# Transposed products of a two-layer hybrid backbone: 512 weight columns per pass over four open PSUM tiles, in place of 256 over one

## The chip, the cores and the metric

One core of a Trainium2 chip runs the whole program. The metric is device time of one execution in microseconds (us); a lower time is better. The trace is one execution taken by the hardware profiler; TensorE is PE in its rows (its weight loads PEld), VectorE DVE, ScalarE ACT, GpSimd POOL and SyncE SP. "ACTq" is ACT's instruction queue, which also issues DMAs; each engine's queue is worked in the order in which it was written.

## The reference

512 tokens (256 of context, 256 latent), width 1024, two layers, each followed by a squared-ReLU MLP. Cut to what the change touches:

```
layer 0:  z, xbc, dt, q, k, v, lr, r = split(h @ w_in)
          y = ssd_scan(x, dt, B, C) both directions        # 16 heads of 64, chunks of 128 tokens
          o = gla_scan(q, k, v, gate) both directions      # 8 heads
          y = rmsnorm((y + D*x) * silu(z));  o = rmsnorm(o) * silu(r)
          out = concat(y, o) @ w_out
layer 1:  q, i, f, g, u = split(h @ w_in)
          o = gla_scan(silu(q), 1 - f, v = i, log f) both directions; s5 on u
          o = rmsnorm(o) * silu(g) ...
```

The change concerns z, v and r of layer 0, and v and g of layer 1: five products whose result is wanted with tokens on the partitions.

## The kernel before, in words

All weights come from HBM as fp32. `wtile` (line 210) loads a block of 512 KB into one of four buffers from the SP queue and splits it into a high part (`whi`, ACT, line 79) and a rest (`wlo`, DVE, line 86); `mm3` (line 100) then spends three matmuls on each pair of blocks: high by high, high by rest, rest by high. The activations `hhi`, `hlo` are split likewise.

There are two forms of product. `gemm_f` (line 319) holds a 128x128 block of weights in the array and moves 512 token columns. `gemm_t` (line 338), the one of this change, holds a block of activations (128 contraction rows by 128 tokens) and moves weight columns, so tokens come out on the partitions. Before, it takes 256 weight columns at a time: two weight blocks of four contraction tiles each, and for each pair of token blocks one PSUM tile (`psd`, a pool of four tiles of 128x512), whose halves are two token blocks of 256 columns. The whole contraction runs for one tile, `put` empties it, and the next tile follows. A product of 1024 columns for 512 tokens is 4 chunks of 96 matmuls; all five together are 1728 matmuls of 256 columns.

The order on each engine is made when the program is built, by a scheduler that works down the program's text and moves work ahead of what it holds to be late; the text itself interleaves generators. Three stages hold the work of the change:

- **SSD scan of layer 0** (some 160 to 288 us). `v_r_proj` (line 1029) makes v and r, a chunk per step; `run_out` (line 1048) takes one step for every second yield of `scan_out` (line 956). `scan_out` works on 4 chunks of tokens with 4 groups of heads each, 16 groups in all. For a group it fetches two blocks `R[0]`, `R[1]` (256 KB each, the cumulated decays, one for each direction, spread over all partitions) from DRAM by ACT's queue (line 977), adds a bias to `R[1]` with four ACT instructions (line 980), adds another to `R[0]` on DVE (line 981), selects between them into `R[0]` (DVE, line 982), takes the exponential (ACT, line 983), multiplies by the scores `Ssb` (DVE, line 984), and multiplies the result as the stationary operand (line 989). `R[0]` is free after that matmul, `R[1]` after the selection. Each has three buffers in the pool `ssd2`.
- **GLA of layer 0** (to 480 us). `z_proj` (line 1212) makes z; its steps are given out before each of the four pairs of heads by `ZN`. `gla_in` (line 1238) makes q and k by `gemm_f` and the decays and states by a chain over DVE and ACT.
- **HGRN of layer 1** (985 to 1250 us). `projs` (line 1549) places the chunks of q, v and g into slots -2 to 7 by `QP`, `VP` and `GP`.

In r and z, `put` computes silu: a bound on DVE that reads PSUM, three ACT steps of the sigmoid, and a product on DVE that reads the PSUM tile again, so the tile stays open until then.

Of the kernel before, what the change touches and what calls it, by code (L numbers as in the profile page):

```python
# [12 lines left out]
AF = mybir.ActivationFunctionType  # L13
# [4 lines left out]
P = 128  # L18
T = 512
# [9 lines left out]
NID = 8  # L29
DTM = 11  # L30
NF = 2
ZN = 3, 1, 2, 2
ADN = 0, 6, 11, 0
WA = 0, 1
QP = -2, 1, 2, 5
VP = -2, -1, 0, -1
GP = -1, 0, 4, 6
SP = -2, -1, 1, 3, 3, 5


def emit(tc, A, out):
# [18 lines left out]
    def tl(p, shape, tag, dt=F32, bufs=None):  # L60
        kw = dict(tag=tag, name=tag)
        if bufs is not None:
            kw["bufs"] = bufs
        return p.tile(list(shape), dt, **kw)

    def ps_d():
        return tl(pd, [P, T], "psd")
# [17 lines left out]
    def tt(eng, o, a, b, op):  # L85
        eng.tensor_tensor(out=o, in0=a, in1=b, op=op)  # L86

    def ts(eng, o, a, s1, op0, s2=None, op1=None):
        if op1 is None:
            eng.tensor_scalar(out=o, in0=a, scalar1=s1, scalar2=None, op0=op0)  # L90
        else:
            eng.tensor_scalar(out=o, in0=a, scalar1=s1, scalar2=s2, op0=op0, op1=op1)
# [7 lines left out]
    def mm3(o, l, r, start, stop):  # L100
        mm(o, l[0], r[0], start, False)
        mm(o, l[0], r[1], False, False)
        mm(o, l[1], r[0], False, stop)
# [86 lines left out]
    def sigmoid_(buf):  # L190
        act(buf, buf, AF.Exp, scale=-1.0)
        act(buf, buf, AF.Ln, bias=1.0)
        act(buf, buf, AF.Exp, scale=-1.0)
# [16 lines left out]
    def wtile(W, k0, kt, c0, n):  # L210

        raw = tl(wp, [P, kt, n], "wraw", bufs=RAW)
        Q.dma_start(out=raw, in_=W[k0 * P:(k0 + kt) * P, c0:c0 + n].rearrange("(k p) c -> p k c", p=P))
        return wsplit(raw, kt, n)
# [41 lines left out]
    def step(it, n=1):  # L256
        for _ in range(n):
            next(it, None)
# [78 lines left out]

    def gemm_t(W, c0, x, toks, put):

        w = [wtile(W, 4 * i, 4, c0, 256) for i in range(2)]  # L340
        for i, pair in enumerate(toks):
            ps = ps_d()
            for j, tok in enumerate(pair):
                t_ = slice(tok * P, (tok + 1) * P)
                for k in range(8):
                    wk = w[k // 4]
                    mm3(ps[:, 256 * j:256 * j + 256], (x[0][:, k, t_], x[1][:, k, t_]),
                        (wk[0][:, k % 4], wk[1][:, k % 4]), k == 0, k == 7)
            put(i, ps)

    xd = tc.dram_tile([8, P, T], F32, name="xd")
    xd2 = tc.dram_tile([8, P, 256], F32, name="xd2")
# [603 lines left out]
    def scan_out(c, hs):  # L956

        S_ps = ps_s()
        for g in range(4):
            mm(S_ps[:, g * P:(g + 1) * P], bT[:, g, c * P:(c + 1) * P], cT[:, g, c * P:(c + 1) * P])  # L960
        Ssb = tl(s2, [P, 4, P], "Ssb", bufs=1)
        act(Ssb, S_ps.rearrange("p (g i) -> p g i", g=4), AF.Copy)
        sdt = tl(s2, [P, 4, P], "y", bufs=2)
        tt(V, sdt, Ssb, ident.unsqueeze(1).to_broadcast([P, 4, P]), MUL)
        sd = tl(s2, [P, 4, 1], "sd")
        V.tensor_reduce(out=sd, in_=sdt, axis=mybir.AxisListType.X, op=ADD)
        dsk = tl(s2, [P, 4, 4], "dsk")
        tt(V, dsk, dtm[:, c, 32:48].rearrange("p (g h) -> p g h", g=4), sd.to_broadcast([P, 4, 4]), MUL)
        dsk = dsk.rearrange("p g h -> p (g h)")
        tt(V, dsk, dsk, dskip, ADD)  # L970
        for hf in range(2):
            yI = ps_s()
            for g in (2 * hf, 2 * hf + 1):
                R = []
                for d in range(2):
                    R.append(tl(s2, [P, 4, P], f"R{d}", bufs=3))
                    S.dma_start(out=R[d], in_=acd[d, 4 * g:4 * g + 4, c * P:(c + 1) * P].partition_broadcast(P))
                X = R[0]
                for h_ in range(4):
                    act(R[1][:, h_], R[1][:, h_], AF.Identity, bias=lnd[:, c, 32 + 4 * g + h_:33 + 4 * g + h_])  # L980
                tt(V, X, X, bcol(lnd, c, 4 * g, 4, P), ADD)
                V.copy_predicated(X, ms.bitcast(I32).unsqueeze(1).to_broadcast([P, 4, P]), R[1])
                act(X, X, AF.Exp)
                tt(V, X, X, Ssb[:, g].unsqueeze(1).to_broadcast([P, 4, P]), MUL)
                for h_ in range(4):
                    hh = 4 * g + h_
                    o_ = (g % 2) * 256 + h_ * 64
                    for q_ in (0, 64):
                        PE.matmul(yI[q_:q_ + 64, o_:o_ + 64], lhsT=X[:, h_, q_:q_ + 64], rhs=xtm[:, c, hh * 64:hh * 64 + 64], start=True, stop=True, skip_group_check=True, tile_position=(0, q_))
                yield  # L990
            xs = xtm[:, c, hf * T:(hf + 1) * T]
            xs3 = xs.rearrange("p (h d) -> p h d", h=8)
            tt(V, xs3, xs3, dsk[:, 8 * hf:8 * hf + 8].unsqueeze(2).to_broadcast([P, 8, 64]), MUL)
            tt(V, xs, xs, yI, ADD)
            for d in range(2):
                if hs[d] is None:
                    continue
                yX = ps_s()
                for g in range(2):
                    gg = 2 * hf + g  # L1000
                    mm(yX[:, 256 * g:256 * g + 256], cT[:, gg, c * P:(c + 1) * P], hs[d][:, gg * 256:gg * 256 + 256])
                t1 = tl(s2, [P, T], "y", bufs=2)
                tt(V, t1.rearrange("p (h d) -> p h d", h=8), yX.rearrange("p (h d) -> p h d", h=8),
                   bcol(eac, c, 32 * d + 8 * hf, 8, 64), MUL)
                tt(V, xs, xs, t1, ADD)

    def silu_ps(pl, ps, tag, bufs):

        sg = tl(pl, [P, T], tag, bufs=bufs)
        ts(V, sg, ps, -44.0, MAX)  # L1010
        sigmoid_(sg)
        tt(V, sg, sg, ps, MUL)
        return sg

    PAIRS = ((0, 1), (2, 3))

    def two(t):
        return t.rearrange("p (t c) -> p t c", t=2)
# [8 lines left out]

    ad = counted(ada_all(lambda: scr[0](), (0, 1), (0, 2)))
    def v_r_proj():
        for ch in range(4):  # L1030
            def put(i, ps, ch=ch):
                act(vtm[:, 2 * i:2 * i + 2, 256 * ch:256 * ch + 256], two(ps), AF.Copy)
            gemm_t(W0, 4128 + 256 * ch, h, PAIRS, put)
            yield
        for ch in range(4):
            def put(i, ps, ch=ch):
                sg = sr[:, 2 * i:2 * i + 2, 256 * ch:256 * ch + 256]
                ts(V, sg, two(ps), -44.0, MAX)
                sigmoid_(sg)
                tt(V, sg, sg, two(ps), MUL)  # L1040
            gemm_t(W0, 5184 + 256 * ch, h, PAIRS, put)
            yield

    fill = v_r_proj()
    f1 = state(0, 0, None)
    b1 = state(1, 1, None)
    step(fill)
    def run_out(c, hs):
        for i, _ in enumerate(scan_out(c, hs)):
            if i % 2 == 1:  # L1050
                step(fill)

    f2 = state(0, 1, f1)
    b2 = state(1, 0, b1)
# [155 lines left out]
    osq = tl(g1, [P, 4, 8], "osq")  # L1210

    def z_proj():
        for g in range(4):
            def put(i, ps, g=g):
                sg = silu_ps(g2, ps, "sg", 1)
                ys = xtm[:, 2 * i:2 * i + 2, 256 * g:256 * g + 256]
                tt(V, ys, ys, two(sg), MUL)
                for j in range(2):
                    S.activation(out=sg[:, 256 * j:256 * j + 256], in_=ys[:, j], func=AF.Square,
                                 accum_out=ssq[:, 2 * i + j, g:g + 1])  # L1220
            gemm_t(W0, 256 * g, h, PAIRS, put)
            yield
        rstd_small(ssq, 256)
        for c in range(4):
            y3 = xtm[:, c].rearrange("p (g f) -> p g f", g=4)
            tt(V, y3, y3, ssq[:, c].unsqueeze(2).to_broadcast([P, 4, 256]), MUL)
        yield
# [258 lines left out]
        tt(V, q_, q_, two(ps), MUL)  # L1486

    def v_proj(ch):
        def put(i, ps):
            act(vtm[:, 2 * i:2 * i + 2, 256 * ch:256 * ch + 256], two(ps), AF.Copy)  # L1490
        gemm_t(W1i, 1024 + 256 * ch, h, PAIRS, put)

    def g_proj(ch):
        def put(i, ps):
            g_ = sgl[:, :, 256 * ch:256 * ch + 256]
            ts(V, g_, two(ps), -44.0, MAX)
            sigmoid_(g_)
            tt(V, g_, g_, two(ps), MUL)
        gemm_t(W1i, 4096 + 256 * ch, h, ((2, 3),), put)

    def hgrn_in(hd_):
        def chain(d):
# [45 lines left out]

    def projs(slot):
        for f_, at in ((q_proj, QP), (v_proj, VP), (g_proj, GP)):  # L1550
            for ch in range(4):
                if at[ch] == slot:
                    f_(ch)
        for a_ in SP:
            if a_ == slot:
                step(s5)
# [137 lines left out]
```

## Time and profile before

| | us |
|---|---|
| median of 3 runs (1477.54 to 1480.27) | 1480.12 |
| the profiled execution | 1479.99 |
| its span, first to last instruction | 1478.3 |
| PE busy | 1424.7 (96%) |
| DVE busy | 945.8 (64%) |
| ACT busy | 682.5 (46%) |
| POOL busy | 328.0 (22%) |

1.7 us of the profiled execution lie around the span. Busy PE is not PE at its peak: a matmul counts from its start to its modelled end, and neighbours overlap, so the pace is read from counts in a stretch. The mean granted clock over the span is 0.988.

### The profile page before, as it was taken

The page shows a single profiled execution, that of the slowest core. Times are in us where ns is not written, and L with a number is a line of the kernel's source. Part 1 is how long each engine was busy: PE and PEld are TensorE (multiplying, and loading weights), DVE is VectorE, ACT ScalarE, POOL GpSimd, SP SyncE. Part 2 cuts the span into 40 slices and gives each one's busy share as a digit, 9 for nine tenths or more (in the row PEclk, how much of TensorE's full clock was granted, in tenths as well). Part 3 has the DMA queues.
Part 4 walks back from the last instruction along what each step waited for, and adds up shares of the span by engine and source line. Part 5 has one row for each costly group of instructions (what it writes and reads, how often), then busy time and mean ns, then how long its engine had stood idle before and what let it go on. Part 6 is the DMA issues. An engine that isn't in the chain of part 4 may idle for free.

```text
span 1478.3 us, 24336 instructions
## 1 busy us (share of the span) xinstructions
PE 1424.7 (96%) x9598; PEld 1211.4 (82%) x9598; DVE 945.8 (64%) x1600; ACT 682.5 (46%) x1313; POOL 328.0 (22%) x348
## 2 busy tenths in 40 slices
PE   7999999999989999999999999999999999999998
PEld 4788998888636889877877777899988888899998
DVE  4798688886755447745444834384786898655543
ACT  4566545475433235421322413362375687555532
POOL 2100000000000012394087840213511110044210
PEclk9999999999988999999999999999999999999999
DMA  9732545322266443465567566569645322565752
GB/s 332 193 100 72 139 121 138 93 58 72 97 220 181 143 114 84 150 186 172 156 202 210 171 193 183 148 207 192 172 115 146 113 93 68 156 188 170 208 177 84
DMA packets 291406, 222.43 MB, mean 150 GB/s; under 512 B 22646, under 2 KB 268844, under 8 KB 291292
## 3 DMA queue, kind: packets, MB, share of 16 engines
q1 hardware_dynamic: 253584, 184.84, 42.8%
q10 hardware_dynamic: 32140, 16.09, 4.6%
q0 software_dynamic: 5568, 19.96, 4.3%
q8 instruction: 75, 1.23, 0.4%
q14 instruction: 39, 0.32, 0.1%
HBM read 206.39 MB, written 14.46 MB: 149 GB/s over the span
## 4 chain that ended last, share of the span: by engine, by line
PE 68%; DVE 10%; DMA 8%; issue 5%; ACT 4%; POOL 3%; ACTq 0%; SPq 0%; DVEq 0%; POOLq 0%
PE psd L98 57%; PE pss L98 6%; DMA R<-acd 3%; PE pss L235 3%; PE pss L106 2%; DVE wlo L86 2%; DMA araw<-in_ada_w_dram 1%; DMA wraw<-in_ada_w_dram 1%; POOL cma L86 1%; DVE hL L134 1%; POOL cmb L86 1%; ACT whi L79 1%; DMA wraw<-in_ssd_gla_w_in_dram 1%; ACT hL L79 1%; POOL ph L86 1%
## 5 line engine op out<-in xcount | busy, mean ns | idle before, releaser
L86 DVE TENSOR_TENSOR wlo<-wraw,whi 128x1024 fp32r<-128x1024 f32 (+1 forms) x238 | 308.4, 1299 | 200.9 <-ACT whi L79 199.4
L79 ACT ACTIVATE whi<-wraw 128x1024 fp32r<-128x1024 f32 (+1 forms) x250 | 260.6, 1044 | 342.8 <-DMA wraw<-in_mlp_w_dram 164.6
L98 PE MATMUL psd<-hhi,wlo 128*128 128x512 f32 (+1 forms) x1112 | 381.7, 345 | 1.0 <-DVE wlo L86 1.0
L98 PE MATMUL psd<-hlo,whi 128*128 128x512 f32 (+1 forms) x1112 | 381.7, 345 | 0.8 <-DVE hlo L86 0.8
L98 PE MATMUL psd<-hhi,whi 128*128 128x512 f32 (+1 forms) x1112 | 379.8, 347 | 2.7 <-ACT hhi L79 2.7
L98 PEld LDWEIGHTS psd<-hhi,whi 128*128 128x128 f32 x1112 | 210.2, 191 | 35.7 <-ACT mr L79 5.0
L98 PEld LDWEIGHTS psd<-hhi,wlo 128*128 128x128 f32 x1112 | 211.8, 191 | 25.9 <-DVE wlo L86 2.4
L98 PEld LDWEIGHTS psd<-hlo,whi 128*128 128x128 f32 x1112 | 211.5, 191 | 24.7 <-DVE hlo L86 1.5
L98 PE MATMUL psd<-wlo,hhi 128*128 128x256 f32 x576 | 165.2, 287 | 2.8 <-DVE wlo L86 2.8
L98 PE MATMUL psd<-whi,hhi 128*128 128x256 f32 x576 | 164.9, 288 | 0.0
L98 PE MATMUL psd<-whi,hlo 128*128 128x256 f32 x576 | 164.5, 286 | 0.0
L98 PEld LDWEIGHTS psd<-wlo,hhi 128*128 128x128 f32 x576 | 111.1, 193 | 4.7 <-DVE wlo L86 3.0
L98 PEld LDWEIGHTS psd<-whi,hhi 128*128 128x128 f32 x576 | 110.7, 193 | 2.6 <-issue 1.3
L98 PEld LDWEIGHTS psd<-whi,hlo 128*128 128x128 f32 x576 | 111.0, 193 | 0.6 <-issue 0.2
L98 PE MATMUL psd<-hidh,whi 128*128 128x512 f32 (+1 forms) x288 | 107.7, 374 | 0.0
L98 PE MATMUL psd<-hidh,wlo 128*128 128x512 f32 (+1 forms) x288 | 105.7, 367 | 1.1 <-DVE wlo L86 1.1
L86 POOL TENSOR_TENSOR nsa<-nsa,nsq 128x256 f32<-128x256 f32 x28 | 26.0, 930 | 362.3 <-ACT nsq L79 361.9
L98 PE MATMUL psd<-hidl,whi 128*128 128x512 f32 (+1 forms) x288 | 105.6, 367 | 0.0
L95 DVE SCALAR_TENSOR_TENSOR xtm<-psd,mod,xtm 128x256 f32<-128x256 f32 x96 | 42.3, 476 | 72.4 <-PE psd L98 65.1
L98 PE MATMUL psd<-hl,whi 128*128 128x256 f32 x256 | 73.0, 285 | 0.0
L98 PE MATMUL psd<-hh,wlo 128*128 128x256 f32 x256 | 72.9, 285 | 0.0
L98 PE MATMUL psd<-hh,whi 128*128 128x256 f32 x256 | 72.4, 283 | 0.0
(438 smaller groups left out, 2475.1 us busy)
## 6 DMA issues: line engine op xcount, KB each, us to landing
wraw<-in_mlp_w_dram SPq DMA_DIRECT2D x128, 512.0 KB, 4.2
wraw<-in_ada_w_dram SPq DMA_DIRECT2D x80, 512.0 KB, 3.8
wraw<-in_ssd_gla_w_in_dram SPq DMA_DIRECT2D x48, 512.0 KB, 4.5
wraw<-in_hgrn_s_w_in_dram SPq DMA_DIRECT2D x43, 512.0 KB, 4.3
araw<-in_ada_w_dram SPq DMA_DIRECT2D x16, 512.0 KB, 11.3
R<-acd ACTq DMA_DIRECT2D x32, 256.0 KB, 4.6
wraw<-in_ssd_gla_w_out_dram SPq DMA_DIRECT2D x16, 512.0 KB, 4.7
wraw<-in_hgrn_s_w_out_dram SPq DMA_DIRECT2D x12, 384.0 KB, 3.2
```

The costliest lines, as they stand in the source:

```text
L79: ins = S.activation(out=out_, in_=in_, func=func, scale=scale, bias=bias)
L86: eng.tensor_tensor(out=o, in0=a, in1=b, op=op)
L95: eng.scalar_tensor_tensor(out=o, in0=a, scalar=s, in1=b, op0=op0, op1=op1)
L98: PE.matmul(o, lhsT=l, rhs=r, start=start, stop=stop, skip_group_check=True)
L106: PE.transpose(o, i, ident[:rows, :rows])
L134: V.tensor_tensor_scan(out=o, data0=rz[:n], data1=x, initial=0.0, op0=MUL, op1=ADD)
L235: PE.matmul(ps[32 * gg:32 * gg + 32], lhsT=cs[:, k], rhs=raw[:, g * T:(g + 1) * T], start=(k == 0), stop=(k == 7), skip_group_check=True, ...
```

## The change

`gemm_t` opens one PSUM tile for each token block (four, or two for g, which is for the latent tokens only), takes the contraction in four parts of two tiles with 512 weight columns, and goes over all token blocks with each part; a tile is handed to `put` in the last part. It is a generator that yields after each part, so v and r now have 16 steps in place of 8, and `run_out` takes one at each yield. The number and size of the weight loads stay (40 of 512 KB).

r's gate copies the PSUM tile to `sr` with ACT and finishes from SBUF with a tile `sg` of its own (two buffers in the pool `ssd2`); z's gate multiplies `xtm` by the PSUM tile before the sigmoid is ready and by the sigmoid afterwards. `R[0]` and `R[1]` go from three buffers each to two. The tables of steps and slots change with the number of chunks.

```diff
-ZN = 3, 1, 2, 2
+ZN = 4, 4, 1, 0
-VP = -2, -1, 0, -1
-GP = -1, 0, 4, 6
+VP = -2, -1
+GP = 0, 4
     def gemm_t(W, c0, x, toks, put):
-        w = [wtile(W, 4 * i, 4, c0, 256) for i in range(2)]
-        for i, pair in enumerate(toks):
-            ps = ps_d()
-            for j, tok in enumerate(pair):
+        pss = [ps_d() for _ in toks]
+        for q in range(4):
+            w = wtile(W, 2 * q, 2, c0, T)
+            for i, tok in enumerate(toks):
                 t_ = slice(tok * P, (tok + 1) * P)
-                for k in range(8):
-                    wk = w[k // 4]
-                    mm3(ps[:, 256 * j:256 * j + 256], (x[0][:, k, t_], x[1][:, k, t_]),
-                        (wk[0][:, k % 4], wk[1][:, k % 4]), k == 0, k == 7)
-            put(i, ps)
+                for k in range(2):
+                    kk = 2 * q + k
+                    mm3(pss[i], (x[0][:, kk, t_], x[1][:, kk, t_]), (w[0][:, k], w[1][:, k]), kk == 0, kk == 7)
+                if q == 3:
+                    put(i, pss[i])
+            yield
...
-                    R.append(tl(s2, [P, 4, P], f"R{d}", bufs=3))
+                    R.append(tl(s2, [P, 4, P], f"R{d}", bufs=2))
...
+            def put(i, ps):
+                sg = tl(s2, [P, T], "sg", bufs=2)
+                ts(V, sg, ps, -44.0, MAX)
+                act(sr[:, i, c5], ps, AF.Copy)
                 sigmoid_(sg)
-                tt(V, sg, sg, two(ps), MUL)
+                tt(V, sr[:, i, c5], sr[:, i, c5], sg, MUL)
...
-    step(fill)
+    step(fill, 2)
     def run_out(c, hs):
-        for i, _ in enumerate(scan_out(c, hs)):
-            if i % 2 == 1:
-                step(fill)
+        for _ in scan_out(c, hs):
+            step(fill)
...
+                sg = tl(g2, [P, T], "sg", bufs=1)
+                ys = xtm[:, i, T * ch:T * ch + T]
+                ts(V, sg, ps, -44.0, MAX)
+                tt(V, ys, ys, ps, MUL)
+                sigmoid_(sg)
+                tt(V, ys, ys, sg, MUL)
```

What the scheduler makes of it is seen in two places. The first is PE's queue at the end of the SSD scan. Before, the products of the 16 groups (`pss<-xtm,R`, line 989; the numbers tell the buffers apart) have projection work (`psd`) between them to the end; here are the last two groups:

```order
L98 MATMUL psd<-hlo,whi 128x512
L98 MATMUL psd<-hhi,wlo 128x512
L989 MATMUL pss<-xtm,R_2827 64x64 x8
L98 MATMUL pss<-H_2249,cT 128x256 x2
L98 MATMUL pss<-H_1556,cT 128x256
L989 MATMUL pss<-xtm,R_2847 64x64 x8
L98 MATMUL pss<-H_1556,cT 128x256
L98 MATMUL psd<-whi,hhi 128x256
```

In the changed kernel's queue, from the ninth group on:

```order
L98 MATMUL psd<-wlo,hhi 128x512
L98 MATMUL psd<-whi,hlo 128x512
L991 MATMUL pss<-xtm,R_2040 64x64 x8
L98 MATMUL pss<-H_1495,cT 128x256 x2
L98 MATMUL pss<-H_2014,cT 128x256 x2
L991 MATMUL pss<-xtm,R_2090 64x64 x8
L991 MATMUL pss<-xtm,R_2183 64x64 x8
L98 MATMUL pss<-H_1495,cT 128x256 x2
L98 MATMUL pss<-H_2014,cT 128x256 x2
L98 MATMUL pss<-cT,bT 128x128 x4
L991 MATMUL pss<-xtm,R_2237 64x64 x8
L991 MATMUL pss<-xtm,R_2316 64x64 x8
```

The remaining four groups follow in the same way, and only behind the sixteenth come further matmuls on `psd`: the last eight groups have no projection work between them.

The second place is ACT's queue for the same groups (here with buffer numbers; `R0` and `R1` are `R[0]` and `R[1]`, DMA is the issue of a copy). Before, the copies of three `R0` buffers stand together, a good way ahead of the instructions that need them:

```order
L977 DMA R0_1763<-acd_142 128x4x128 [waits DVE_49,PE_49]
L977 DMA R0_1918<-acd_142 128x4x128 [waits DVE_49,PE_49]
L977 DMA R0_1938<-acd_142 128x4x128 [waits DVE_49,PE_49]
L79 ACTIVATE R0_1763<-R0_1763 128x512 [waits DVE_49]
L977 DMA R1_2081<-acd_142 128x4x128 [waits Activation_49]
```

In the changed kernel, groups 11 to 13 (`R0_2183`, `R0_2237`, `R0_2316`):

```order
L79 ACTIVATE R0_2040<-R0_2040 128x512 [waits DVE_49]
L979 DMA R1_2185<-acd_142 128x4x128
L79 ACTIVATE R1_2185<-R1_2185,lnd_1400 128x128 [waits DMAHW3_49]
L79 ACTIVATE R1_2185<-R1_2185,lnd_1400 128x128 x3
L79 ACTIVATE Ssb_2030<-pss_2025 128x512 [waits PE_49]
L79 ACTIVATE R0_2090<-R0_2090 128x512 [waits DVE_49]
L979 DMA R1_2239<-acd_142 128x4x128 [waits DMAHW5_49]
L79 ACTIVATE R1_2239<-R1_2239,lnd_1400 128x128 [waits DMAHW5_49]
L79 ACTIVATE R1_2239<-R1_2239,lnd_1400 128x128 x3
L979 DMA R0_2183<-acd_142 128x4x128 [waits DVE_49,PE_49]
L979 DMA R0_2237<-acd_142 128x4x128 [waits DMAHW7_49,DVE_49,PE_49]
L79 ACTIVATE R0_2183<-R0_2183 128x512 [waits DVE_49]
```

A copy of an `R1` now stands directly ahead of the instructions that read it, and the copies of the two `R0` stand behind those.

## Rows read from the trace of the kernel before

**Rows 1.** The page: busy time by engine, and the chain that ended last.
```profile
PE 1424.7 (96%) x9598; PEld 1211.4 (82%) x9598; DVE 945.8 (64%) x1600; ACT 682.5 (46%) x1313; POOL 328.0 (22%) x348
...
PE 68%; DVE 10%; DMA 8%; issue 5%; ACT 4%; POOL 3%; ACTq 0%; SPq 0%; DVEq 0%; POOLq 0%
```

**Rows 2.** Windows: us, each engine's busy time (instructions), PEclk, DMA share, GB/s.
```profile
500.00:520.00 20.00, 20.00 (x91) 16.57 (x90) 8.73 (x13) 3.33 (x4) 0.00 (x0) 1.00 0.49 152
196.00:286.00 90.00, 85.61 (x761) 77.61 (x760) 76.12 (x122) 44.61 (x90) 0.99 (x2) 0.98 0.50 133
286.00:375.00 89.00, 86.16 (x634) 75.99 (x633) 64.07 (x95) 54.89 (x133) 0.00 (x0) 0.98 0.23 66
1017.00:1053.00 36.00, 36.00 (x342) 33.95 (x339) 24.58 (x28) 10.87 (x13) 25.13 (x31) 1.00 0.84 189
```

**Rows 3.** Chain of waits, 134 to 196 us: start us, us, what.
```profile
145.68 8.26 PE psd L98 x69
```

**Rows 4.** Tile R: ns min/median/max, first and last start us.
```profile
L989 PE MATMUL pss<-xtm,R x256: 221/222/271, 196.1 to 285.1; 128*64 128x64 f32 x128
L79 ACT ACTIVATE R<-R,lnd x64: 384/388/404, 167.1 to 267.6; 128x128 f32<-128x128 f32 x64
...
L86 DVE TENSOR_TENSOR R<-R,lnd x16: 679/684/693, 165.1 to 278.5; 128x512 f32<-128x512 f32 x16
L982 DVE COPY_PREDICATED R<-ms,R x16: 719/736/757, 169.5 to 280.9; 128x512 f32<-128x512 int32 x16
L79 ACT ACTIVATE R<-R x16: 614/630/633, 170.3 to 281.6; 128x512 f32<-128x512 f32 x16
L86 DVE TENSOR_TENSOR R<-R,Ssb x16: 672/682/692, 192.9 to 283.3; 128x512 f32<-128x512 f32 x16
...
DMA to landing us min/median/max: 3.2/4.6/9.8
```

**Rows 5.** Chain of waits, 196 to 270 us: copies of R that bound it.
```profile
196.83 4.98 DMA R<-acd
...
205.62 3.40 DMA R<-acd
...
251.79 6.89 DMA R<-acd
```

**Rows 6.** Waits, 196 to 286 us: who <- whom: us in total, times, longest.
```profile
ACT R L79 <- DVE R L982: 33.2, 8, 10.1
DVE R L86 <- DMA R<-acd: 8.8, 4, 4.5
```

**Rows 7.** Timeline of ACT in the SSD scan: start us, us, instructions.
```profile
196.83 2.51 ACTq L977 DMA_DIRECT2D R<-acd  x3
...
209.04 0.40 ACT L79 ACTIVATE R<-R,lnd 128x128 f32<-128x128 f32 x1 [2.80 <-DMA R<-acd]
209.24 0.37 ACTq L977 DMA_DIRECT2D R<-acd  x1
...
273.36 0.37 ACTq L977 DMA_DIRECT2D R<-acd  x1
```

**Rows 8.** Windows of 2 us: us, PE busy (matmuls), PEclk, DMA share, GB/s.
```profile
236.00:238.00 2.00, 1.56 (x14) 1.00 0.76 153
238.00:240.00 2.00, 0.00 (x0) 1.00 0.04 12
240.00:242.00 2.00, 1.63 (x6) 0.81 0.01 4
242.00:244.00 2.00, 2.00 (x9) 0.50 0.00 0
```

**Rows 9.** Groups of instructions, 196 to 286 us: xcount | busy us, mean ns.
```profile
L79 ACT ACTIVATE sr<-sr 128x512 f32<-128x512 f32 x24 | 14.8, 623 | 1.8 <-DVE sr L90 1.3 <-ACT sr L79 0.3
```

**Rows 10.** Chain of waits in GLA: one DVE step of its first chain.
```profile
302.09 1.21 DVE gc L134
```

**Rows 11.** Chain of waits at the start of HGRN.
```profile
1017.50 22.14 PE psd L98 x183
```

More of the change, by code (lines that the diff above doesn't have):

```diff
@@ L1005, in scan_out @@
                 tt(V, xs, xs, t1, ADD)
[L1007 to L1015, printed above, removed]
+    ALL = (0, 1, 2, 3)
     def two(t):
@@ L1029, in v_r_proj @@
     def v_r_proj():
[L1030 to L1038, printed above, removed]
+        for ch in range(2):
+            c5 = slice(T * ch, T * ch + T)
+            yield from gemm_t(W0, 4128 + T * ch, h, ALL, lambda i, ps: act(vtm[:, i, c5], ps, AF.Copy))
+        for ch in range(2):
+            c5 = slice(T * ch, T * ch + T)
+            def put(i, ps):
+                sg = tl(s2, [P, T], "sg", bufs=2)
+                ts(V, sg, ps, -44.0, MAX)
+                act(sr[:, i, c5], ps, AF.Copy)
                 sigmoid_(sg)
-                tt(V, sg, sg, two(ps), MUL)
-            gemm_t(W0, 5184 + 256 * ch, h, PAIRS, put)
-            yield
+                tt(V, sr[:, i, c5], sr[:, i, c5], sg, MUL)
+            yield from gemm_t(W0, 5184 + T * ch, h, ALL, put)
     fill = v_r_proj()
@@ L1212, in z_proj, with put @@
     def z_proj():
[L1213 to L1217, printed above, removed]
+        for ch in range(2):
+            def put(i, ps, ch=ch):
+                sg = tl(g2, [P, T], "sg", bufs=1)
[4 more added lines that the diff above has]
+                tt(V, ys, ys, sg, MUL)
                 for j in range(2):
[L1219 to L1222, printed above, removed]
+                    S.activation(out=sg[:, 256 * j:256 * j + 256], in_=ys[:, 256 * j:256 * j + 256], func=AF.Square,
+                                 accum_out=ssq[:, i, 2 * ch + j:2 * ch + j + 1])
+            yield from gemm_t(W0, T * ch, h, ALL, put)
         rstd_small(ssq, 256)
@@ L1488, in v_proj @@
     def v_proj(ch):
-        def put(i, ps):
-            act(vtm[:, 2 * i:2 * i + 2, 256 * ch:256 * ch + 256], two(ps), AF.Copy)
-        gemm_t(W1i, 1024 + 256 * ch, h, PAIRS, put)
+        drain(gemm_t(W1i, 1024 + T * ch, h, ALL, lambda i, ps: act(vtm[:, i, T * ch:T * ch + T], ps, AF.Copy)))
     def g_proj(ch):
         def put(i, ps):
-            g_ = sgl[:, :, 256 * ch:256 * ch + 256]
-            ts(V, g_, two(ps), -44.0, MAX)
+            g_ = sgl[:, i, T * ch:T * ch + T]
+            ts(V, g_, ps, -44.0, MAX)
             sigmoid_(g_)
-            tt(V, g_, g_, two(ps), MUL)
-        gemm_t(W1i, 4096 + 256 * ch, h, ((2, 3),), put)
+            tt(V, g_, g_, ps, MUL)
+        drain(gemm_t(W1i, 4096 + T * ch, h, (2, 3), put))
     def hgrn_in(hd_):
@@ L1550, in projs @@
         for f_, at in ((q_proj, QP), (v_proj, VP), (g_proj, GP)):
-            for ch in range(4):
+            for ch in range(len(at)):
                 if at[ch] == slot:
```

## The prediction, made before the changed kernel ran

> **What bounds the kernel now.** I read the page first: PE is busy for 96% of the span and the chain that ended last runs over PE for 68% of it, so in the large PE decides, and a change that saves PE time should show [rows 1]. Then I cut the windows at the stages in which the changed products stand. In the SSD scan, 196 to 286 us, PE is busy 85.61 of 90 us and DVE 76.12; in GLA after it PE is busy 86.16 of 89, in HGRN's first part 36.00 of 36 [rows 2]. But the chain inside the SSD scan is not PE's alone. It goes again and again through copies of R, 3.4 to 6.9 us each [rows 5]. ACT's waits there are mostly for the selection into R (33.2 us in 8 waits), and DVE waits 8.8 us for the copies themselves [rows 6]. At 196.83 three copies of `R[0]` leave together, a little over half a us after the first product of the ring started at 196.1: they were held up by the buffers [rows 4, 7]. So this stage now stands near a balance: the ring of R turns just fast enough, because projection matmuls fill PE between the products.
>
> **The matmuls.** A narrow transposed matmul takes 8.26 / 69 = 0.120 us [rows 3]; 512 columns take 20 / 91 = 0.220 us [rows 2]. Two narrow ones (0.240) become one wide one (0.220), so 1728 narrow become 864 wide and PE's work falls by 207.4 - 190.1 = 17 us. That is the most it can give, where PE ends last throughout.
>
> **The SSD scan.** v and r are 768 of the 1728. PE's queue has 403 narrow ones ahead of the first group's product now, 263 wide ones in the changed kernel: 57.9 against 48.4 us, so the first product starts 9.5 us later, at 205.6 against 196.1 [rows 4]. From there the ring decides. An `R[0]` is bound by: copy (landing 3.2 to 9.8, median 4.6 us), sum, selection, exponential and product with the scores at some 0.6 to 0.75 us each, product on PE, next copy [rows 4]. Its turn as it really runs is longer, since each step stands in a queue: the copies at 196.83 serve groups 4 to 6, the one at 273.36 group 16 [rows 7], so four turns took 76.5 us, 19.1 us each, and with three buffers that is 6.4 us a group. With two buffers one turn serves two groups, and the queue order makes copies leave late.
>
> I walk it by the order of ACT's and DVE's queues, with a landing of 4.6. Groups 3 and 4: copies out at 206, products at 217 and 219. Groups 5 and 6: their copies stand on ACT behind eight bias steps whose own copies left at 215 to 217, so they leave at 222 and land at 227; behind other DVE steps of 0.6 us the products come at 235 and 240, the second one because its exponential stands behind the bias steps of group 7. Groups 7 and 8: out at 244 and 247, behind group 8's bias steps and the sigmoid steps of r; products at 257 and 264. Group 9: copy at 261, exponential at 270. That is 64 us from the first product, 3.4 turns of the old length.
>
> From there to the last product the order leaves nothing ahead. A copy of an `R[1]` stands directly before the bias steps that wait for it, and copies of `R[0]` behind those. A copy behind bias steps does leave soon after they start, 209.24 against 209.04 [rows 7]. Following the queue, eight landings come strictly one after the other: `R[1]` of 11, `R[1]` of 12, `R[0]` of 11 with 12, `R[1]` of 13, `R[1]` of 14 with `R[0]` of 13, `R[1]` of 15 with `R[0]` of 14, `R[1]` of 16, `R[0]` of 16. Between them lie 12 us: 0.3 to 0.7 us before each of the next copies that waits only for a place, some 2 us (sum, selection, dispatch) behind each of the three `R[0]`, and 3.9 us from the last landing to the product. A copy alone on the queue landed in 3.4 us, three at once in 5.0 [rows 5]; there is little weight traffic in this tail, so I take 4.0: 8 x 4.0 + 12 = 44 us (37.6 with 3.2, 52 with 5.0). The last product then comes at 205.6 + 64 + 44 = 313.6 against 285.1: **+28.5 us**. PE has no projection work of its own for the tail, since the next `psd` matmuls stand behind group 16.
>
> One page has a price for such a copy: the Trainium skill, DMA: Bandwidth & Descriptors, section Anatomy of one DMA, gives about 2.0 us plus the bytes at 436 GB/s, fitted for copies issued by GpSimd: an estimate of 2.6 us for 256 KB. With it the tail would be 33 us and the whole 1489; the row has 3.2 as its least and 4.6 as its median, and I go by the row.
>
> **Behind the scan.** z is 384 narrow (46.1 us), all behind the last group now. In the changed order 24 wide ones stand before the ninth group and 168 (37.0 us) behind the last: -9.1. Against that, GLA's first chain (three ACT steps, then DVE, with a scan of 1.21 us [rows 10], 6 to 9 us in all) has 24 wide matmuls, 5.3 us, in front of its first transposes; before there were 121 narrow ones, 14.5 us. I put 3 us on that (1 to 4): **-6 us**.
>
> HGRN's v and g go from 576 narrow to 288 wide. 240 of these stand ahead of the first HGRN chain, where PE runs without a gap (183 matmuls in 22.14 us [rows 11]; 36.00 of 36 us [rows 2]): 240 x 0.020 = **-5 us**; the other 48, among DVE and ACT work, I put at nothing.
>
> **PE's clock.** Around 239 us PE had nothing for 0.44 + 2.0 + 0.37 = 2.8 us, and the granted clock went to 0.50, the lower of its two levels [rows 8]. In the tail PE does some 15 us of small work in 44, so I expect the half clock there and at the start of z: 3 us (0 to 5): **+3 us**.
>
> **At nothing.** r's extra PSUM copies (8 steps on ACT, like those of 0.62 us in [rows 9]) lie in ACT's queue, busy 44.6 of 90 [rows 2], and the walk counts them. DVE's steps keep their number. Weight loads keep their number and size. Four open tiles take the whole pool, but 18 wide matmuls, 4 us, lie between a tile's end and its next use, and `put` now needs only a bound and a copy; were `put` late by more, PE would wait for it at each chunk.
>
> **Sum.** +28.5 - 6 - 5 + 3 = +20.5 on the profiled execution of 1479.99, which lies 0.1 under the median: **1500 us**. Its own range is 1487 (landing 3.2, all credits whole) to 1515 (landing 5.0 and half of the credits).
>
> **Rivals.** *Two buffers are enough and PE decides.* PE's own work from the first group on is 193 wide matmuls (42.5 us) and what is left of today's 85.61 after 365 narrow and 48 wide ones, 31.2: 73.7 us, so the last product could come at 279, and all three places save: 1463 us. For it: PE is nearly full in this stage today [rows 2]. Against: the three held copies and the 33.2 us [rows 6, 7], and a queue that leaves the last eight groups bare. Chance 0.13. The Trainium skill, Trainium Kernel Development and Optimization, section Best Practices, says to double-buffer so that DMA and compute overlap, which would put two where the kernel had three; by that rule it is this case. The copies held with three buffers speak against the rule here [rows 7].
>
> *The ring turns faster than I walk it.* What decides is the mean turn: seven turns lie between the first and the last pair, and if they take less than 12.5 us each, the end at 205.6 + 88 = 293 is made up by the credits behind it (+8 - 11 + 3). With 12 us: 1479 to 1480. Chance 0.10.
>
> *The ring keeps its old turn to the end.* Seven times 19.1 us put the last product at 339, +54: 1528 us. Against: from group 9 on the sigmoid steps and weight splits are gone from both queues. Chance 0.08.
>
> **The chances.** Forecast 0.69, the rivals 0.13, 0.10 and 0.08. Slower by over 0.2% (3 us, about what a measurement of this kernel can tell from no change): 0.77; within it 0.10; faster 0.13. The range reaches from 1474, between the first two rivals, to 1516, the top of the forecast's own.
>
> **What would show it.** The first product of R near 206 and the last near 314 in the tile's view; R's landings at the head of the waits there, far over 8.8 us for DVE; PE busy under half between 270 and 312, with a granted clock of 0.5 in part of it; 864 matmuls of 512 columns with `whi` as the moving operand at 0.220; HGRN reached 20 to 26 us later than now. Wrong would be: the last product before 293; PE above nine tenths busy until it; or, with the scan as forecast, a stretch elsewhere that changes by more than 10 us.

## The result, and the profile after

| | us |
|---|---|
| the changed kernel, median of 8 runs (1488.16 to 1514.19) | 1490.16 |
| the kernel before, median of 8 runs beside them | 1478.18 |
| ratio, with its 95% interval | 1.0075 [1.0049, 1.0100] |
| the prediction | 1500, range 1474 to 1516 |

The change makes the kernel slower by some 12 us. The first traced execution of it took 1514.19 us, 1.6% above the median, so the rows of after are those of a later one (run e9 below, span 1492.9 us, ratio 1.0100 [1.0067, 1.0133]).

The page: busy time, and the chain that ended last.

```profile
PE 1418.9 (95%) x8734; PEld 1167.9 (78%) x8734; DVE 948.1 (64%) x1600; ACT 687.9 (46%) x1321; POOL 330.6 (22%) x348
...
PE 72%; DVE 12%; DMA 7%; ACT 4%; POOL 3%; issue 2%; ACTq 0%; SPq 0%; DVEq 0%; POOLq 0%
```

PE has 864 matmuls and 6 us of busy time less than in [rows 1], and the span is 14.6 us longer. Where that lies is read from the first and last instructions of some tiles:

| us | before | after | after is late by |
|---|---|---|---|
| first product of R | 196.1 | 204.9 | 8.8 |
| last product of R | 285.1 | 305.8 | 20.7 |
| last step of GLA (DVE, `vtm` by `osq`) | 478.9 | 488.5 | 9.6 |
| first product on `U` (s5, ahead of HGRN) | 1014.5 | 1025.9 | 11.4 |
| first bound on `hE` (DVE, HGRN's first chain) | 1065.1 | 1082.4 | 17.3 |
| transposes of HGRN's last head | 1244.4 | 1260.4 | 16.0 |
| end of the span | 1478.3 | 1492.9 | 14.6 |

**The scan.** Tile R after, which answers to [rows 4] (columns as there):

```profile
L991 PE MATMUL pss<-xtm,R x256: 222/222/369, 204.9 to 305.8; 128*64 128x64 f32 x128
...
DMA to landing us min/median/max: 3.2/3.8/6.9
```

The windows of the scan after (columns as in [rows 2]), first with and then without projection work between the products:

```profile
206.00:270.00 64.00, 58.70 (x341) 46.75 (x337) 51.35 (x77) 39.10 (x78) 0.00 (x0) 1.00 0.49 131
270.00:306.00 36.00, 20.16 (x169) 15.93 (x169) 26.87 (x47) 10.99 (x29) 0.98 (x2) 0.67 0.26 78
```

To 270 PE is nearly as full as before [rows 2]; from there it is busy 20.16 of 36 us, at a mean granted clock of 0.67, and no engine is full. What bounds it stands in the chain of waits, 262 to 307 us (start us, us, what):

```profile
263.46 3.60 DMA R<-acd
...
270.32 1.04 PE pss L991 x16
...
274.54 0.64 PE pss L991 x16
...
275.20 3.17 DMA R<-acd
...
280.35 1.14 PE pss L991 x16
...
281.51 4.36 DMA R<-acd
...
287.96 4.55 DMA R<-acd
...
297.49 1.15 PE pss L991 x16
...
298.66 3.17 DMA R<-acd
```

The ninth group's product is the one at 270.32. After it a product frees its buffer and at once a copy leaves, at 275.20, 281.51 and 298.66: the loop of R without cover. Five landings, 18.85 us together, lie in the chain shown; four of them, 15.25 us, come behind the ninth product.

**HGRN.** DVE's timeline before (start us, us, instruction), ahead of the first bound on `hE`:

```profile
1056.80 3.39 DVE L665 TENSOR_TENSOR_SCAN xs<-ph,xs 128x768 f32<-128x768 f32 x2
...
1063.92 1.12 DVE L86 TENSOR_TENSOR sp<-xa,xb 64x384 f32<-64x384 f32 x2
1065.07 0.76 DVE L90 TENSOR_SCALAR hE<-hE 128x512 f32<-128x512 f32 x2
```

and after:

```profile
1065.90 1.23 DVE L86 TENSOR_TENSOR wlo<-wraw,whi 128x1024 fp32r<-128x1024 f32 x1 [4.45 <-ACT whi L79]
1067.05 1.75 DVE L667 TENSOR_TENSOR_SCAN xs<-ph,xs 128x768 f32<-128x768 f32 x1
1068.80 1.23 DVE L86 TENSOR_TENSOR wlo<-wraw,whi 128x1024 fp32r<-128x1024 f32 x1
1069.94 2.59 DVE L667 TENSOR_TENSOR_SCAN xs<-ph,xs 128x768 f32<-128x768 f32 x1
...
1079.38 1.11 DVE L86 TENSOR_TENSOR sp<-xa,xb 64x384 f32<-64x384 f32 x2
...
1082.39 0.76 DVE L90 TENSOR_SCALAR hE<-hE 128x512 f32<-128x512 f32 x2
1083.06 0.68 DVE L86 TENSOR_TENSOR sgl<-sgl,psd 128x512 f32<-128x512 f32 x1
...
1085.67 0.68 DVE L86 TENSOR_TENSOR sgl<-sgl,psd 128x512 f32<-128x512 f32 x1
```

In both, steps of s5 (`xs`, `sp`: the scan that runs beside HGRN) stand ahead of the chain's first step in DVE's queue. After the change weight splits and g's gate (`sgl`) stand among them, and the first split has waited 4.45 us for ACT. HGRN's first step on DVE comes 56.5 us after the first product on `U`, where it came after 50.6.

ACT and PE after the change, at the same place:

```profile
1064.81 1.06 ACT L79 ACTIVATE whi<-wraw 128x1024 fp32r<-128x1024 f32 x1 [4.43 <-POOL xs L86]
...
1079.50 0.63 ACT L79 ACTIVATE sgl<-sgl 128x512 f32<-128x512 f32 x1 [2.57 <-DVE sgl L90]
1080.03 1.07 ACT L79 ACTIVATE hE<-psd 128x512 f32<-128x512 f32 x2
```

```profile
1080.66 0.80 PE L98 MATMUL psd<-hhi,whi 128*128 128x512 f32 x1 [4.83 <-ACT hE L79]
```

ACT's split, for which DVE waited, had itself waited 4.43 us for s5's work on POOL. PE ended its matmuls for `hE` at 1065 and those for g at 1076, but ACT's first step on `hE`, at 1080.03, stands behind g's sigmoid, which waits for the bound on `sgl` on DVE. Until then the two tiles of g, which the gate reads again at 1083.06 and 1085.67, and the two of `hE` are all open, and these four are the whole pool `psd`: PE waits 4.83 us for ACT to read one of them. Before the change PE had no wait there (busy 36.00 of 36 us from 1040 to 1076).

### The profile page after: what moved, and what is told of

Its sections match the earlier page's. It is cut to its first block, busy times and chain, and to the rows that moved or that the text cites. A ratio compares the mean times of both kernels' runs of the same rounds, so it can differ in the third digit from the quotient of the medians.

```text
span 1512.5 us, 22632 instructions
## 1 busy us (share of the span) xinstructions
PE 1438.2 (95%) x8734; PEld 1179.4 (78%) x8734; DVE 949.5 (63%) x1600; ACT 688.1 (45%) x1321; POOL 333.7 (22%) x348
## 4 chain that ended last, share of the span: by engine, by line
PE 78%; DVE 10%; DMA 5%; ACT 4%; issue 2%; POOL 0%; ACTq 0%; SPq 0%; DVEq 0%
PE psd L98 64%; PE pss L98 7%; PE pss L235 3%; PE pss L106 2%; DMA R<-acd 2%; DMA wraw<-in_ada_w_dram 1%; DVE wlo L86 1%; ACT whi L79 1%; DVE ke L86 1%; ACT hL L79 1%; DVE nxh L86 1%; DVE xtm L86 1%; DMA xt<-in_x_dram 1%; DVE hL L134 1%; DVE hlo L86 0%
## 5 line engine op out<-in xcount | busy, mean ns | idle before, releaser
L98 PE MATMUL psd<-whi,hhi 128*128 128x512 f32 x288 | 112.0, 401 | 2.5 <-ACT sr L79 2.5
L98 PE MATMUL psd<-wlo,hhi 128*128 128x512 f32 x288 | 113.7, 395 | 0.0
L98 PE MATMUL psd<-whi,hlo 128*128 128x512 f32 x288 | 112.8, 393 | 0.0
L98 PEld LDWEIGHTS psd<-hidh,whi 128*128 128x128 f32 x288 | 54.3, 189 | 20.5 <-issue 8.3
L98 PEld LDWEIGHTS psd<-whi,hhi 128*128 128x128 f32 x288 | 54.6, 190 | 16.1 <-ACT sr L79 3.3
L235 PE MATMUL pss<-wraw,cs 128*32 128x512 f32 x320 | 57.6, 651 | 5.8 <-DMA wraw<-in_ada_w_dram 5.8
## 6 DMA issues: line engine op xcount, KB each, us to landing
araw<-in_ada_w_dram SPq DMA_DIRECT2D x16, 512.0 KB, 11.4
```

The source lines that it names most:

```text
L98: PE.matmul(o, lhsT=l, rhs=r, start=start, stop=stop, skip_group_check=True)
L235: PE.matmul(ps[32 * gg:32 * gg + 32], lhsT=cs[:, k], rhs=raw[:, g * T:(g + 1) * T], start=(k == 0), stop=(k == 7), skip_group_check=True, ...
```

## The experiments

Each ratio is to runs of the kernel before on the same chip, at the same time.

**e1, e9: the changed kernel again.**

> The changed kernel as it is, for a trace of one more execution. Theory (the ring of two R buffers): first product of R at 206, last at 304 to 308, then less time than before in GLA and HGRN, so that HGRN begins some 12 to 17 us later than before; about 1489 us. Rival (something spread over the program): the lag against before grows in steps outside the scan.

> The changed kernel once more, timed beside the two others of this call. Both theories expect its ratio to the kernel before again, 1.005 to 1.010.

One execution (e1) took 1494.12 us with the products of R from 205.1 to 305.5; the timed runs (e9) gave 1.0100 [1.0067, 1.0133]. The stage times of both agree within 1.4 us.

**e2: three buffers of R.**

```diff
-R.append(tl(s2, [P, 4, P], f"R{d}", bufs=2))
+R.append(tl(s2, [P, 4, P], f"R{d}", bufs=3))
...
-sg = tl(s2, [P, T], "sg", bufs=2)
+sg = sr[:, i, c5]
 ts(V, sg, ps, -44.0, MAX)
-act(sr[:, i, c5], ps, AF.Copy)
 sigmoid_(sg)
-tt(V, sr[:, i, c5], sr[:, i, c5], sg, MUL)
+tt(V, sg, sg, ps, MUL)
```

> Wide products, but R[0] and R[1] have three buffers again and r's gate is the old one (no tile sg, the PSUM tile stays open until the last product), so the same SBUF. Theory (the ring): the last product of R comes at 276 to 288 in place of 306, and the whole falls to 1463 to 1472 us, below both kernels. Rival (the wide order with four open tiles is what holds the scan): the last product stays past 300 and the time within 5 us of 1490.

**e3: two buffers, but the old gate** (only the second part of that diff).

> Wide products, two buffers of R as in the changed kernel, but r's gate the old one (no copies by ACT, the PSUM tile open to the end). Theory (the ring): within 6 us of the changed kernel, 1484 to 1496, since the ring is the same and the eight copies cost ACT some 5 us at most. Rival (the gate's extra ACT copies in the queue ahead of the bias steps are the price): 1470 to 1480.

**e4: the kernel before with two buffers of each R** (3 to 2, nothing else).

> The kernel before with one thing changed: R[0] and R[1] have two buffers. Theory (the ring): the last product moves from 285 to 297 to 312 and the time rises by 10 to 25 us, to 1488 to 1503. Rival (narrow matmuls in smaller pieces fill the ring's waits): within 4 us of before.

The products of R in e2, e3 and e4:

```profile
L991 PE MATMUL pss<-xtm,R x256: 222/222/369, 209.2 to 298.1; 128*64 128x64 f32 x128
```

```profile
L991 PE MATMUL pss<-xtm,R x256: 222/222/369, 205.2 to 308.9; 128*64 128x64 f32 x128
```

```profile
L989 PE MATMUL pss<-xtm,R x256: 221/222/370, 195.2 to 305.0; 128*64 128x64 f32 x128
```

Ratios: e2 1.0058 [1.0040, 1.0076], e3 1.0150 [1.0129, 1.0171], e4 1.0082 [1.0048, 1.0117]. Two buffers alone, without one wide matmul, put the last product at 305.0, where the changed kernel has it; that part of the theory stands. In e4 PE has work while the ring turns (busy 72.73 of 74 us from 196 to 270, with projection work between the products), and the ring still ends late, so the turn with two buffers costs by itself. Of its 19.9 us, 12.2 come back: 507 matmuls on `psd` stand between the first and the last product, where there were 414, and GLA then takes 181.6 us from the last product in place of 193.8. e2 and e3 differ by the buffers alone, and their ratios by 0.009, about e4's loss. e3 took 1496.07 us: at the edge of its theory, 2 us more than e1 on the same chip; its rival (1470 to 1480) falls.

But e2 was to come to 1463 to 1472 and came to 1485.22: with three buffers the products still take 88.9 us (89.0 before), only 13 us later, and the kernel stays slower than before. So the buffers are not the whole loss.

**e5: a third buffer for `R[0]` alone.**

```diff
-R.append(tl(s2, [P, 4, P], f"R{d}", bufs=2))
+R.append(tl(s2, [P, 4, P], f"R{d}", bufs=3 - d))
...
-sg = tl(s2, [P, T], "sg", bufs=2)
+sg = tl(s2, [P, T], "sg", bufs=1)
```

> The changed kernel with a third buffer for R[0] alone (R[1] keeps two, the new gate keeps its own tile, now one buffer of it). Theory: the ring that held the scan is R[0]'s, because an R[0] buffer is held through selection, exponential, product and matmul while R[1]'s is free after the selection; then the last product of R comes at 285 to 298 (305.5 in the changed kernel, 298.1 with three of each and the old gate), and the time is 1.002 to 1.006 of the kernel before. Rival: R[1]'s copies, which stand right ahead of the bias steps that wait for them, set the pace; then the third R[0] changes nothing, last product 302 to 308 and a ratio of 1.007 to 1.012.

```profile
L991 PE MATMUL pss<-xtm,R x256: 222/222/271, 205.2 to 290.0; 128*64 128x64 f32 x128
```

Ratio 1.0039 [1.0009, 1.0069]: both numbers are the theory's, by which the ring that bounds the changed scan is that of `R[0]`, whose buffer is held from its copy to the product. Two things limit this: with the buffer back, the scheduler again puts projection work between the last products, so the run shows the two together; and a third buffer for `R[1]` alone was not tried.

**e10: the copies from POOL's queue.**

```diff
-S.dma_start(out=R[d], in_=acd...)
+G.dma_start(out=R[d], in_=acd...)
```

> The changed kernel with the copies of R[0] and R[1] issued from POOL's queue, which has nothing else to do in this stage; two buffers each as in the change. Theory: part of the ring's turn is the place of a copy in ACT's queue, behind the bias steps of an earlier group that wait for their own landing, so that eight landings of 3.1 to 4.9 us stand one after the other at the end; from a queue of their own the copies leave when their buffer is free, the last product of R comes at 291 to 300 (305.5 in the changed kernel) and the time falls by 3 to 9 us. Rival: the turn is made of the landing and the five steps behind it whoever issues; then the last product stays within 302 to 309 and the time within 2 us.

```profile
L991 PE MATMUL pss<-xtm,R x256: 222/222/370, 205.0 to 308.3; 128*64 128x64 f32 x128
...
DMA to landing us min/median/max: 3.6/4.2/7.2
```

Ratio 1.0154 [1.0112, 1.0197]. The theory falls: the end does not come earlier. The rival had the last product right (302 to 309) but not the time, which grew by 7 us. A copy also landed later from here (median 4.2 us against 3.8) and its issue took 0.75 us of POOL against 0.37 us on ACT, so the run does not show that the place in ACT's queue costs nothing; it shows no gain from another queue.

**e6: wide products in layer 0 alone, three buffers, old gate** (e2 with v and g of layer 1, `VP` and `GP` as before).

> Wide products for v, r and z only, with three buffers for R[0] and R[1] and the old gate of r; v and g of layer 1 as in the kernel before. Theory: the wide products of layer 1 cost some 4 us where the prediction gave them -5 (with three of each R and everything wide, the lag on the kernel before was 1.4 us at the start of the last MLP stage of layer 0 but 5 us at the end); then this run ends where that lag stood: a ratio of 1.000 to 1.003, and the stages from HGRN on have their old lengths. Rival, the prediction's term: layer 1 saves 5 us, so this kernel must lose them and comes to a ratio of 1.008 to 1.010.

**e7: wide products in layer 1 alone** (the kernel before with the change's `v_proj`, `g_proj`, `VP` and `GP`).

> The kernel before with only v and g of layer 1 made wide, in the slots of the change. Theory: the first decay of HGRN (hE) starts some 8 to 11 us later because g's two open tiles, its gate and the weight splits stand ahead of it, of which about half is caught up by the end of HGRN, and 4 us are lost at HGRN's end where g no longer fills; ratio 1.002 to 1.005. Rival, the prediction's term: 240 wide matmuls ahead of the first chain save 5 us, ratio 0.996 to 0.998.

**e8: only v of layer 1 wide** (g narrow, in its four old slots).

> The kernel before with only v of layer 1 wide; g stays narrow, in its four old slots. Theory: what layer 1 loses is g's (its place ahead of the first decay, and the missing fill at the end), so v alone saves its 384 x 0.120 - 192 x 0.220 = 3.8 us: ratio 0.996 to 0.999, first hE near 1057, the end of HGRN 2 to 4 us earlier. Rival: four open PSUM tiles at once, v's, hold up what follows; then the first hE comes after 1062 and the ratio is 1.000 to 1.004.

Ratios: e6 1.0026 [0.9999, 1.0053], e7 1.0031 [1.0002, 1.0061], e8 1.0017 [0.9981, 1.0052]. The intervals reach to no change or, for e7, almost, so the stage times have to decide. In four traces with narrow layer 1 (before, e4, e6, e12) the first bound on `hE` comes 50.2 to 51.4 us after the first product on `U`; in five with all of layer 1 wide (e1, e2, e5, e7, e9) it comes after 56.5 us each time. From there to the transposes of the last head are 179.3 to 181.3 us in the four and 176.5 to 177.9 in the five, and from these to the end of the span 232.1 to 233.9 in all nine. From `U` to these transposes it is 229.5 to 232.7 us in the four and 233.0 to 234.4 in the five: wide v and g cost about 3 us there in the mean, and the longest of the four, e6, comes within 0.3 us of the five. In each of the five PE waits 4.8 us for ACT's step on `hE`, as shown above; in the four no wait of PE at this place is longer than 0.9 us. In the windows before (columns as in [rows 2]) and after, PE has run out of work at HGRN's end, behind DVE:

```profile
1233.00:1243.00 10.00, 7.34 (x62) 6.20 (x61) 9.53 (x22) 7.00 (x23) 0.00 (x0) 1.00 0.41 122
```

```profile
1244.00:1254.00 10.00, 5.65 (x34) 5.05 (x35) 9.93 (x21) 5.61 (x17) 0.00 (x0) 0.80 0.40 121
```

e6 has the old lengths (51.4 and 181.3 us) and e7 the new ones (56.5 and 177.6), as the theory had it, with g's gate and tiles ahead of `hE`. In e8 the bound comes even later, 61.7 us after `U`, with the first `hE` on ACT at 1066.0, and PE waits 5.43 us, for the tile of the narrow g: there the rival's times come true, and g's width alone is not at fault; wide v does it too.

**e11: v's second half behind the first chain** (e8 with `VP = -2, 1`).

> The kernel before with v of layer 1 wide as in the run with v alone, but its second half (heads 4 to 7) placed in slot 1 and not in slot -1, so that 96 wide matmuls come behind the first HGRN chain and not ahead of it. Theory: HGRN is bound by the chains of DVE and ACT from the first decay on, and what the wide products save ahead of it is given back as PE's idle time at HGRN's end; with the second half behind, the first hE starts 15 to 25 us earlier relative to the first product on U (45 us in the kernel before, 58 with v alone), PE's idle slice at the end goes, and the ratio is 0.992 to 0.997. Rival: four open tiles of psd hold up HGRN's own products wherever v stands; then PE waits for psd in slot 1 and the ratio is 1.000 to 1.006.

Ratio 1.0086 [1.0051, 1.0120], and neither account foresaw it. Tile `hE` of e11: ACT's first step on it, and the bound on DVE behind it.

```profile
L79 ACT ACTIVATE hE<-psd x16: 574/580/609, 1055.7 to 1236.3; 128x512 f32<-128x512 f32 x16
...
L90 DVE TENSOR_SCALAR hE<-hE x16: 400/420/2290, 1068.4 to 1238.8; 128x512 f32<-128x512 f32 x16
```

Its waits, 1055 to 1092 us:

```profile
ACT hL L79 <- DVE hE L90: 12.0, 1, 12.0
PEld psd L98 <- ACT whi L79: 10.0, 1, 10.0
PE psd L98 <- ACT whi L79: 9.6, 1, 9.6
```

PE and ACT did reach the chain early (41 us after `U`), but the bound stood behind s5's scan on DVE and came 12.7 us later, 53.5 after `U`. Meanwhile ACT waited 12.0 us in its queue ahead of the next weight split, and PE 9.6 us for that split; from `U` to the last head's transposes it is 241.4 us, 11.5 more than before. This is what binds HGRN's start here: DVE's queue, with s5 ahead of the chain. Moving that step of s5 behind the first chain was not tried.

**e12: z alone wide** (the kernel before with the change's `z_proj` and `ZN`).

> The kernel before with only z wide (its gate and its steps as in the change); v and r of layer 0, three buffers of R and all of layer 1 as before. Theory: in the scan nothing is changed (last product of R at 283 to 287), and behind it PE is full enough that z's 384 x 0.120 - 192 x 0.220 = 3.9 us come off GLA: from the last product of R to the end of GLA 184 to 188 us where the runs with the old z had 187 to 194, ratio 0.996 to 0.998: of the five products z alone is worth making wide, and this kernel beats both. Rival: GLA's own chains of DVE and ACT set its end, as HGRN's did, and the saved time is given back as idle PE; then GLA's length stays at 187 to 194 and the ratio is 0.999 to 1.003.

Ratio 0.9985 [0.9960, 1.0010]: faster than the changed kernel, but not shown to be faster than the kernel before. Its scan ended 1 us earlier than expected (281.9). GLA took 200.1 us from there, longer than either account has it, so the trace decides between neither of them; the last section shows its clock.

## Why the prediction came out as it did

The sign and the main place were right, but three terms were off: two were forecast too high by some 8 us each, the third too low by 9 to 10. They partly cancel, so that the total came as near as it did (+20.5 us forecast, +12 in the medians, +14.6 in the trace) is in part luck.

- **First product and first half: right.** 205.6 was forecast and 204.9 measured, though with the measured price of a wide matmul (below) the same sum gives 207.4. The ninth group's exponential was forecast at 270 and came at 268.8. The walk along the queues held for eight groups, to within 5 us.
- **The tail: mechanism right, size too large.** "Eight landings come strictly one after the other", 8 x 4.0 + 12 = 44 us from 270 to 313.6; the last product came at 305.8, 35.5 us behind the ninth. Four landings of 3.17 to 4.55 us, 15.25 together, lie in the chain there and not eight (32); the others ran beside them. What lies between took 20.2 us and not 12. The landing itself was well chosen (3.8 in the median). The Trainium skill, DMA: Bandwidth & Descriptors, section Anatomy of one DMA, gave the estimate of 2.6 us; no copy here landed in under 3.1 us (the least, in e3), and those issued by GpSimd, as in the page's fit, not under 3.6 (e10), so the traces do not agree.
- **Behind the scan: -6 and +3 for the clock, measured -11.1** (9.6 late at GLA's end, 20.7 at the scan's). The 3 us for a bare first chain were not needed: GLA's first DVE scan comes 5.8 us behind the last product after the change (311.6 against 305.8), and came 13.0 behind it before (298.1 against 285.1). The -6 was worked out from the wide z, but e4 has as short a GLA (181.6 us) with narrow z, and e5 and e12 a long one (194.1 and 200.1) with wide z: the number is not shown to be z's. Part of the 11.1 may be the clock's, which differs from run to run in this stage (last section).
- **The matmuls: 0.227, not 0.220.** The chain ahead of the first product has

```profile
189.23 6.36 PE psd L98 x28
198.20 6.81 PE psd L98 x30
```

  which are 0.227 us each. The window that I divided by its count had shorter matmuls in it and counted those that reach in over its ends. Two narrow ones at 0.120 against 0.227 save 0.013 and not 0.020 us: 11 us in all for the five products, not 17.
- **HGRN: wrong, -5 forecast, +4.5 measured** (11.4 late at `U`, 16.0 at the last head's transposes). The step that failed is "240 of these stand ahead of the first HGRN chain, where PE runs without a gap: 240 x 0.020". A full PE was taken for the bound. But the chain's first step stands in DVE's queue behind s5, weight splits and g's gate; e11 shows it by bringing ACT there 4.7 us earlier than before (40.8 us after `U`) and having the bound 2.9 us later (53.5). And the open tiles were put at nothing, with "were `put` late by more, PE would wait for it"; here `put` was late, and PE waited 4.83 us, about the size of the loss.
- **The signs that were named.** The clock did fall to 0.50 (294 to 300 us). PE was busy for 56% of the bare tail, not under half; DVE's waits for landings were 10.7 us, not far over 8.8; HGRN was reached 11 to 17 us late, not 20 to 26. GLA's 11.1 us are a stretch elsewhere that changed by over 10; with the scan as forecast, that would have been a sign against the prediction.
- **Two sums.** The low end of the forecast's own range, 1487, does not follow from its terms: 22.1 - 9.1 - 5 is +8, or 1488, at the least. The old turn kept to the end gives +54 - 6 - 5 + 3, or 1526, not 1528. Neither changes the forecast.
- **The rivals.** Two buffers are not enough: e4 says so without any other part of the change, 1.0082 [1.0048, 1.0117]. The rule of the Trainium skill, Trainium Kernel Development and Optimization, section Best Practices, to double-buffer for overlap, does not carry over to this ring, where the third buffer was worth 19.9 us of scan (285.1 against 305.0 for the last product), 7.7 of them left at GLA's end. The ring turned faster than I walked it, but the end came at 305.8 and not at the 293 from which that would have decided.

By the ratios, wide products in layer 0 with three buffers cost 1.0026 (e6), those of layer 1 1.0031 (e7), and both together 1.0058 (e2): they add up, though each interval is about 0.003 to either side and that of e6 reaches below 1. With two buffers in place of three e2 becomes e3, 1.0150. The changed kernel's 1.0075 to 1.0100 would then leave some 0.005 to the new gate; but e1, on the chip of e3, was only 2 us faster than e3, so that part is not shown. Three buffers with wide v and r (e2, e6) start the products of R at 209.2 and 210.3, 4 to 5 us behind the changed kernel. PE waits 2.3 and 2.5 us ahead of them for ACT to empty a tile of `psd` into `vtm`, where the changed kernel has no wait from 134 us on: there, too, the open tiles put at nothing cost time. The same 328 matmuls of e2 then take 72.9 us busy in place of 70.9, at a mean granted clock of 0.98 against 1.00.

## What to carry to other kernels

A full PE does not make PE the bound: look in the trace for the first instruction of the next stage on every engine, and ask what stands ahead of it in that engine's queue, and whether PE's next tile will be free. Before buffers are cut, follow one buffer through its whole loop (copy, steps, product, next copy), and ask what covers that loop when the filler runs out; here the filler went ahead and the tail stood bare, and even with filler the turn with two buffers was too long (e4). Divide a window by its count only where all instructions in it are of one shape.

## What was not expected of the hardware

**The clock in GLA differs between runs of the same instructions.** From the last product of R to GLA's end, before and e8 have the same work in layer 0 (columns as in [rows 2]); before:

```profile
285.30:479.20 193.90, 182.70 (x1241) 133.62 (x1240) 127.94 (x193) 95.55 (x268) 0.00 (x0) 0.95 0.39 123
```

and e8:

```profile
283.60:470.90 187.30, 175.64 (x1236) 129.80 (x1235) 127.05 (x192) 95.57 (x268) 0.00 (x0) 0.98 0.40 125
```

The stretch is 6.6 us shorter at a mean granted clock of 0.98 against 0.95. In e12, with less work, it took 200.20 us at 0.89:

```profile
282.10:482.30 200.20, 191.00 (x1044) 125.63 (x1043) 127.91 (x192) 96.29 (x268) 0.00 (x0) 0.89 0.38 118
```

and there the clock fell in slices in which PE counted as busy throughout:

```profile
358.00:373.00 15.00, 15.00 (x79) 10.79 (x78) 11.36 (x15) 9.01 (x34) 0.00 (x0) 0.96 0.00 0
373.00:388.00 15.00, 15.00 (x56) 11.19 (x54) 11.37 (x17) 6.98 (x21) 0.00 (x0) 0.81 0.00 1
```

So a difference of a few us in GLA between two traces says little; what set it off was not found.

**A DVE step and a POOL step, each longer beside the other.** In the trace after, an s5 step on DVE takes twice its time while a weight split runs on POOL:

```profile
1072.46 2.69 DVE L86 TENSOR_TENSOR xd<-xs,ph 128x384 f32<-128x384 f32 x1
```

```profile
1071.57 3.17 POOL L86 TENSOR_TENSOR wlo<-wraw,whi 128x1024 fp32r<-128x1024 f32 x1 [0.65 <-ACT whi L79]
```

Before, the same step took 1.32 us (at 1060.12), and another split on POOL after the change 2.39 (at 1060.46). A bound on `hE` reaches 2281 ns after the change, where its longest was 428 before. The Trainium skill, SBUF — State Buffer, section SBUF: two separate sides, says that these two engines share a pair of ports under an exclusive lock, which one instruction holds to its end while the other waits. That one of them pays for the other would fit; but here both rows are longer, by 1.37 and 0.78 us, and the DVE step ends 0.41 us behind the split, too soon for 1.32 us of work that began at the split's end. No run isolated it. It may be part of why s5's steps take longer ahead of HGRN when more stands beside them.
